# Forgetting attention's logits: two float32 heads side by side against stacked float32r halves

## The chip, the cores and the metric

The kernel runs on one core of one Trainium2 chip. The metric is the time of one execution on the device in microseconds (us), taken as the median of several runs. One execution was recorded by the hardware profiler; all rows shown come from that one.

## The reference

Four layers work on 256 tokens of width 1024, batch 1: two of a first block (gated linear attention, stick-breaking attention, each with an MLP) and two of a second block. The change lies in the second block, whose layers mix with eight heads of forgetting attention and eight heads of retention, each 64 wide. All data is float32.

```python
def forgetting_attention(q, k, v, f_logit):          # 8 heads of 64, 256 tokens
    log_f = jax.nn.log_sigmoid(f_logit)
    cum = jnp.cumsum(log_f, axis=1).transpose(0, 2, 1)
    ...
    logits = jnp.einsum('bhqd,bhkd->bhqk', qb, k) * HEAD_DIM ** -0.5
    logits = logits + cq[..., :, None] - cum[..., None, :]
    logits = jnp.where(kpos[None, :] <= qpos[:, None], logits, -jnp.inf)
    probs = jax.nn.softmax(logits, axis=-1)
    return jnp.einsum('bhqk,bhkd->bhqd', probs, v)
```

In each layer `u = rms_norm(h)`, `proj = u @ w_in` gives q, k, v, the forget logits and the retention's inputs, and `h + concat(fox, ret) @ w_out` follows.

## The kernel before

**Projections.** Activations lie feature by feature: a tile of 128 partitions holds 128 features of all 256 tokens. Every large product is made from float32r halves: a float32 operand x is split into `hi = float32r(x)` (a copy on ScalarE, ACT) and `lo = x - hi` (a subtraction on VectorE, DVE), and `mm3` (lines 402 to 404) issues three matmuls hi·hi, hi·lo, lo·hi. One call of `proj` walks eight steps k; a step is two output blocks of three matmuls, so six matmuls of 256 columns, and a call is 48. Weights come by DMA on SP's queue; `prep` splits each half of a weight (L330 on ACT, L333 on DVE, 128x1024 each) ahead of its use, in three buffered weights, with its priority pushed back by 150 (`LATER`).

**Hooks.** `proj(..., hooks=...)` calls functions between its steps, which puts small work of the attention between the matmuls of the next projection. `hooked("10 13 22 25", (f0, f1, f2, f3), 4)` says for each function two digits: how many projections after its own it runs, and behind which step. In forgetting attention one projection j (0 to 3) makes q and k of two heads (a pair).

**The order of the work.** The code's order is not the final one. Each instruction gets a priority in the order in which it is written, and when the program is built the framework's scheduler deals out each engine's instructions one after another: among those whose operands it estimates to be ready, the one with the best priority. The order of each engine, TensorE (PE) too, is then fixed, and the engine waits where an operand is later than estimated. `add_manual_dep` is used in places to hold an order against this.

**The pair, stage by stage.** `f0(j)` (L1117, L1118) reads q and k of the pair from PSUM, multiplies by the norm's reciprocal R (and q by -1/8) and writes them as float32 into `foxq`: head 0 in partitions 0 to 63, head 1 in 64 to 127. `f1(j)` (L1128) makes the logits: for each head, queries 0 to 127 against 128 keys and queries 128 to 255 against 256 keys, as float32 matmuls with 64 rows of contraction, the two heads in the two halves of the array's rows. Then come the row minimum of the negated logits with the decay added (L1136, DVE), exponentials with their sums (L396, ACT), the reciprocal and the scaling (L1139, L1141, DVE). `f2(j)` transposes the weights on PE (L1149) and copies them out (L1151, ACT); `f3` at every second pair multiplies by v and splits the result for `w_out`. While the first pair of a layer is worked on, the end of the retention part (`g2(1)`: L508 to L515, L1099, L1100, and the split L467, L468) is still on DVE and ACT.

**Buffers.** `SHARE` groups tile names into rings of buffers; `ga` has three of 640 float32 per partition and holds, among others, `foxl` (the logits); `gd` three of 512 with `foxq`; `gc` two of 512.

Of the kernel before, what the change touches and what calls it, by code (L numbers as in the profile page):

```python
# [11 lines left out]
F32R = mybir.dt.float32r  # L12
AF = mybir.ActivationFunctionType
ALU = mybir.AluOpType

P = 128
T = 256
# [202 lines left out]
class Net:  # L220
# [52 lines left out]

    SHARE = {}
    for _g, _n, _w, _names in (
        ("ga", 3, 640, "glaE sbe foxl relu pleg ffng retsq"),
        ("gb", 2, 640, "glaQ sbsp relu2 lnsq"),
        ("gc", 2, 512, "wa2 wa1 glaG sbh ph"),
        ("gd", 3, 512, "glasq qk foxq rot pl rgr"),
        ("ge", 1, 512, "retb ptin"),  # L280
        ("gf", 4, 384, "retw foxw sbw"),
        ("gg", 2, 512, "rety erz sbl w2 w2l"),
        ("gh", 2, 512, "lnq lnu ffny a1 glaK rgv rga"),
        ("gj", 2, 256, "sq rfv rfa"),
        ("gk", 2, 256, "diag lnvar"),
        ("gl", 2, 512, "lnsum retG"),
        ("gn", 1, 256, "lncm foxg idle"),
        ("go", 1, 256, "ssum foxf"),
        ("gr", 2, 256, "rfr"),
        ("gp", 2, 256, "spread"),  # L290
        ("gq", 1, 512, "retc glagrow"),
    ):
        for _x in _names.split():
            SHARE[_x] = (_g, _n, _w)
# [672 lines left out]
    def pv(self, v, c0, ws):  # L967
# [10 lines left out]
                    self.nc.tensor.matmul(pO[r, i // 2, P:T], v[:, 1, hc], ws[i][:, 256:384], start=False, stop=True, skip_group_check=True)  # L978
        return pO

    def diag0(self, a):

        d = a.rearrange("p (c n) -> p c n", n=P)
        for c in (0, 2):
            self.nc.gpsimd.affine_select(out=d[:, c, :], in_=d[:, c, :], pattern=[[1, P]], compare_op=ALU.is_gt, fill=0.0,
                                         base=0, channel_multiplier=-1)


    def mix2(self, l, x, acc):
        nc = self.nc  # L990
        mm = nc.tensor.matmul
# [14 lines left out]
        for c in range(2):  # L1006
            ps = rps[c]
# [4 lines left out]
        ps = self.proj(f"w_f{l}", 0, x)  # L1012
# [9 lines left out]
                                     op0=ALU.mult, op1=ALU.add)  # L1022

        gd = self.dram.tile([8, T], F32, name=f"cum{l}")
# [87 lines left out]
        fps, fqs, fls, fws = {}, {}, {}, {}  # L1112

        def f0(j):
            ps = fps[j]
            qk = self.t([P, 2, T], "foxq")
            nc.vector.scalar_tensor_tensor(out=qk[:, 0, :], in0=ps[:, 0, :], scalar=-0.125, in1=R, op0=ALU.mult, op1=ALU.mult)  # L1117
            nc.vector.tensor_tensor(out=qk[:, 1, :], in0=ps[:, 1, :], in1=R, op=ALU.mult)  # L1118
            fqs[j] = qk

        def f1(j):
            qk = fqs[j]

            pls = [self.pacc().rearrange("p a b -> p (a b)") for _ in range(2)]
            for a, b in ((0, 128), (128, 384)):
                for i in range(2):
                    r = slice(64 * i, 64 * i + 64)
                    mm(pls[i][:, a:b], qk[r, 0, a:a + P], qk[r, 1, 0:b - a], start=(a == 0), stop=True, skip_group_check=True)  # L1128
            fls[j] = []
            for i in range(2):  # L1130
                pl = pls[i]
                lg = self.t([P, 384], "foxl")
                mx = self.t([P, 2], "foxm")
                sm = self.t([P, 2], "foxs")
                for c, (a, b) in enumerate(((0, 128), (128, 384))):
                    nc.vector.tensor_tensor_reduce(out=lg[:, a:b], in0=pl[:, a:b], in1=fbs[j // 2][:, 2 * j % 4 + i, a:b], scale=1.0, scalar=3e38,  # L1136
                                                   op0=ALU.add, op1=ALU.min, accum_out=mx[:, c:c + 1])
                    self.act(lg[:, a:b], lg[:, a:b], "Exp", scale=-1.0, bias=mx[:, c:c + 1], accum_out=sm[:, c:c + 1])
                nc.vector.reciprocal(sm, sm)  # L1139
                for c, (a, b) in enumerate(((0, 128), (128, 384))):  # L1140
                    nc.vector.tensor_scalar(out=lg[:, a:b], in0=lg[:, a:b], scalar1=sm[:, c:c + 1], scalar2=None, op0=ALU.mult)  # L1141
                fls[j].append(lg)
# [16 lines left out]
        pv = self.proj_tok(f"w_fv{l}", 0, x, hooks=hk)  # L1159
        for c in range(2):  # L1160
            nc.scalar.mul(v[:, c, 0:512], pv[c].rearrange("p a b -> p (a b)"), rt[:, c:c + 1])
        fh = self.hooked("10 13 22 25", (f0, f1, f2, f3), 4)
        for j in range(4):
            fps[j] = self.proj(f"w_fqk{l}", j, x, hooks=([(3, lambda: g2(1))] if j == 0 else []) + fh(j))
        return o, (fh(4), fh(5), ())
# [272 lines left out]
```

## Time and profile before

| | before |
|---|---|
| median of 3 runs | 1303.39 us (1301.37 to 1304.65) |
| the profiled execution's own time | 1302.13 us |
| its span, first to last instruction | 1300.4 us |
| PE busy (matmuls) | 1282.7 us, 99% |
| PE weight loads busy | 1236.5 us, 95% |
| DVE busy | 946.8 us, 73% |
| ACT busy | 750.8 us, 58% |
| granted TensorE clock, mean | 0.998 |
| mean DMA rate | 179 GB/s |

The profiled execution's own time holds 1.7 us beside its span. A matmul's row gives its start and a duration that reaches past the start of the next one, since matmuls are pipelined: what a matmul costs is read from start to start, not from its duration. PEld are the weight loads of the same lines. A row of the timeline merges like instructions that follow each other (x8); in brackets stands how long the engine was idle before it, and what ended that.

### The profile page before, as it was taken

How to read it: one execution, taken by the hardware profiler on the slowest of the kernel's cores; microseconds unless marked ns; L12 is line 12 of the kernel's file. 1: busy time of each engine (PE TensorE's matmuls, PEld its weight loads, DVE VectorE, ACT ScalarE, POOL GpSimd, SP SyncE). 2: the span in 40 equal slices, each digit the busy share in tenths (PEclk: the TensorE clock that was granted, in tenths of full speed). 3: DMA queues.
4: the chain of work that ended last, by engine and by line, in shares of the span. 5: the costliest groups of instructions: out<-in, count | busy, mean ns of one | idle time of the engine just before them, and what ended most of it. 6: DMA issues, size and time to landing. Idle time of an engine off the chain costs nothing.

```text
span 1300.4 us, 25420 instructions
## 1 busy us (share of the span) xinstructions
PE 1282.7 (99%) x10314; PEld 1236.5 (95%) x10314; DVE 946.8 (73%) x1514; ACT 750.8 (58%) x1181; POOL 36.2 (3%) x89
## 2 busy tenths in 40 slices
PE   8999999999999999999999999999999999999997
PEld 6999999999899999999989999999989899999996
DVE  6979855559557955558887788766787869885755
ACT  6556744447776744446746665544674557554544
POOL 0000000000231000000010000000001000000000
PEclk9999999999999999999999999999999999999999
DMA  8654666654533575555654465565657446656561
GB/s 288 217 172 155 193 197 183 189 179 141 185 115 118 171 228 189 185 189 194 215 182 140 138 207 187 183 184 158 220 167 221 141 127 196 192 185 188 170 222 50
DMA packets 64694, 232.78 MB, mean 179 GB/s; under 512 B 7216, under 2 KB 7488, under 8 KB 63936
## 3 DMA queue, kind: packets, MB, share of 16 engines
q1 hardware_dynamic: 61920, 220.75, 54.1%
q10 hardware_dynamic: 2016, 8.28, 1.7%
q0 software_dynamic: 640, 2.11, 0.5%
q8 instruction: 81, 1.33, 0.4%
q14 instruction: 37, 0.30, 0.1%
HBM read 227.96 MB, written 3.16 MB: 178 GB/s over the span
## 4 chain that ended last, share of the span: by engine, by line
PE 90%; DVE 5%; DMA 3%; ACT 2%; issue 1%; POOL 0%; SPq 0%; POOLq 0%; ACTq 0%; DVEq 0%
PE up L402 20%; PE up L403 19%; PE up L404 19%; PE acc L403 9%; PE acc L404 8%; PE acc L402 8%; DVE wl L333 1%; DMA raw<-in_w_pg_dram 1%; PE aux L976 1%; ACT wh L330 1%; DMA wa<-in_w_a_dram 1%; PE aux L586 1%; PE acc L1128 1%; PE acc L1070 0%; DMA raw<-in_w_gv_dram 0%
## 5 line engine op out<-in xcount | busy, mean ns | idle before, releaser
L333 DVE TENSOR_TENSOR wl<-raw,wh 128x1024 fp32r<-128x1024 f32 (+2 forms) x420 | 506.3, 1210 | 257.1 <-ACT wh L330 255.4
L330 ACT CAST wh<-raw 128x1024 fp32r<-128x1024 f32 (+2 forms) x420 | 434.9, 1036 | 387.3 <-PE acc L403 139.2
L402 PE MATMUL up<-b,wh 128*128 128x256 f32 (+1 forms) x2032 | 576.2, 284 | 2.8 <-DVE pleg L1266 1.6
L403 PE MATMUL up<-b,wh 128*128 128x256 f32 (+1 forms) x2032 | 572.4, 282 | 0.2 <-DVE b L527 0.2
L404 PE MATMUL up<-b,wl 128*128 128x256 f32 (+1 forms) x2032 | 569.6, 280 | 0.0
L402 PEld LDWEIGHTS up<-b,wh 128*128 128x128 f32 x2032 | 381.5, 188 | 10.3 <-issue 5.2
L403 PEld LDWEIGHTS up<-b,wh 128*128 128x128 f32 x2032 | 382.8, 188 | 1.2 <-DVE b L527 0.4
L404 PEld LDWEIGHTS up<-b,wl 128*128 128x128 f32 x2032 | 382.9, 188 | 0.2 <-issue 0.2
L403 PE MATMUL acc<-b,wh 128*128 128x256 f32 (+1 forms) x960 | 270.6, 282 | 0.0
L404 PE MATMUL acc<-b,wl 128*128 128x256 f32 (+1 forms) x960 | 270.4, 282 | 0.0
L402 PE MATMUL acc<-b,wh 128*128 128x256 f32 (+1 forms) x960 | 270.2, 281 | 0.0
L402 PEld LDWEIGHTS acc<-b,wh 128*128 128x128 f32 x960 | 181.1, 189 | 0.1
L403 PEld LDWEIGHTS acc<-b,wh 128*128 128x128 f32 x960 | 181.0, 189 | 0.1
L404 PEld LDWEIGHTS acc<-b,wl 128*128 128x128 f32 x960 | 180.7, 188 | 0.1
L402 PE MATMUL up<-wh,b 128*128 128x512 f32 (+1 forms) x136 | 52.9, 393 | 1.6 <-ACT wh L361 1.6
L403 PE MATMUL up<-wl,b 128*128 128x512 f32 (+1 forms) x136 | 51.9, 381 | 0.0
L404 PE MATMUL up<-wh,b 128*128 128x512 f32 (+1 forms) x136 | 51.7, 381 | 0.0
L467 ACT CAST b<-ffny 128x256 fp32r<-128x256 f32 x44 | 17.9, 407 | 54.3 <-DVE ffny L1202 53.4
L402 PEld LDWEIGHTS up<-wh,b 128*128 128x128 f32 x136 | 25.5, 188 | 8.2 <-ACT wh L361 2.3
L404 PEld LDWEIGHTS up<-wh,b 128*128 128x128 f32 x136 | 25.5, 188 | 5.3
L403 PEld LDWEIGHTS up<-wl,b 128*128 128x128 f32 x136 | 25.6, 188 | 4.9 <-DVE wl L362 0.4
L1194 DVE TENSOR_TENSOR glaS<-up,rfr 128x256 f32<-128x256 f32 x44 | 18.7, 425 | 12.4 <-PE up L404 12.3
(257 smaller groups left out, 1151.3 us busy)
## 6 DMA issues: line engine op xcount, KB each, us to landing
raw<-in_w_fu_dram SPq DMA_DIRECT2D x88, 512.0 KB, 4.2
raw<-in_w_mu_dram SPq DMA_DIRECT2D x64, 512.0 KB, 4.1
raw<-in_w_md_dram SPq DMA_DIRECT2D x64, 512.0 KB, 4.2
raw<-in_w_fd_dram SPq DMA_DIRECT2D x32, 512.0 KB, 3.7
raw<-in_w_sqk_dram SPq DMA_DIRECT2D x16, 512.0 KB, 4.1
raw<-in_w_rqk_dram SPq DMA_DIRECT2D x16, 512.0 KB, 4.9
raw<-in_w_fqk_dram SPq DMA_DIRECT2D x16, 512.0 KB, 4.4
raw<-in_w_out_dram SPq DMA_DIRECT2D x16, 512.0 KB, 3.8
```

Of the source, the lines that this page charges most:

```text
L330: i = nc.scalar.copy(hi, r).ins
L333: i = nc.vector.tensor_tensor(out=lo, in0=r, in1=hi, op=ALU.subtract).ins
L402: mm(o, wh, xh, start=first, stop=False, skip_group_check=True)
L403: mm(o, wh, xl, start=False, stop=False, skip_group_check=True)
L404: self.last_mm = mm(o, wl, xh, start=False, stop=last, skip_group_check=True).ins
L467: nc.scalar.copy(out[0][:, i, :], src)
L586: nc.tensor.matmul(ps[:, k, :], ones, s[k][:, i, :], start=(k == 0 and i == 0), stop=(i == 1), skip_group_check=True)
L976: self.nc.tensor.matmul(pO[r, i // 2, :], v[:, 0, hc], ws[i][:, 0:256], start=(i < 2), stop=False, skip_group_check=True)
L1128: mm(pls[i][:, a:b], qk[r, 0, a:a + P], qk[r, 1, 0:b - a], start=(a == 0), stop=True, skip_group_check=True)
L1194: nc.vector.tensor_tensor(out=a[:, 2:], in0=ps[:, 0, :], in1=R, op=ALU.mult)
```

## The change

Each pair's q and k are written as before, in the order k, q, into a tile z. A new function `stack` makes for each of the two heads a tile X of 128 partitions and three slots in float32r: slot 0 has the high half of k in the head's own 64 partitions and the low half in the other 64; slot 1 has the high half of q in both; slot 2 the low half of q in both. A matmul of slot 1 against slot 0 contracts over 128 rows and gives q_hi·k_hi + q_hi·k_lo, one of slot 2 against slot 0 gives q_lo·k_hi + q_lo·k_lo. `f1` sums the two in PSUM, one head after the other. Hooks of f1 and f2 move by one step, and three names change rings.

```diff
-        ("ga", 3, 640, "glaE sbe foxl relu pleg ffng retsq"),
+        ("ga", 3, 768, "glaE sbe stack relu pleg ffng retsq"),
-        ("gc", 2, 512, "wa2 wa1 glaG sbh ph"),
-        ("gd", 3, 512, "glasq qk foxq rot pl rgr"),
+        ("gc", 2, 512, "wa2 wa1 glaG sbh foxq ph"),
+        ("gd", 3, 512, "glasq qk foxl rot pl rgr"),
...
+    def stack(self, z):
+        nc = self.nc
+        Xs = []
+        for i in range(2):
+            r, q = slice(64 * i, 64 * i + 64), slice(64 - 64 * i, 128 - 64 * i)
+            X = self.t([P, 3, T], "stack", F32R)
+            nc.scalar.copy(X[r, 0:2, :], z[r, :, :])
+            nc.vector.tensor_tensor(out=X[q, 0:3:2, :], in0=z[r, :, :], in1=X[r, 0:2, :], op=ALU.subtract)
+            nc.scalar.copy(X[q, 1, :], z[r, 1, :])
+            nc.vector.tensor_tensor(out=X[r, 2, :], in0=z[r, 1, :], in1=X[r, 1, :], op=ALU.subtract)
+            Xs.append(X)
+        return Xs
...
-            qk = self.t([P, 2, T], "foxq")
-            nc.vector.scalar_tensor_tensor(out=qk[:, 0, :], in0=ps[:, 0, :], scalar=-0.125, in1=R, op0=ALU.mult, op1=ALU.mult)
-            nc.vector.tensor_tensor(out=qk[:, 1, :], in0=ps[:, 1, :], in1=R, op=ALU.mult)
-            fqs[j] = qk
+            z = self.t([P, 2, T], "foxq")
+            nc.vector.tensor_tensor(out=z[:, 0, :], in0=ps[:, 1, :], in1=R, op=ALU.mult)
+            nc.vector.scalar_tensor_tensor(out=z[:, 1, :], in0=ps[:, 0, :], scalar=-0.125, in1=R, op0=ALU.mult, op1=ALU.mult)
+            fqs[j] = self.stack(z)
...
-            pls = [self.pacc().rearrange("p a b -> p (a b)") for _ in range(2)]
-            for a, b in ((0, 128), (128, 384)):
-                for i in range(2):
-                    r = slice(64 * i, 64 * i + 64)
-                    mm(pls[i][:, a:b], qk[r, 0, a:a + P], qk[r, 1, 0:b - a], start=(a == 0), stop=True, skip_group_check=True)
+            pls = []
+            for X in fqs[j]:
+                pl = self.pacc().rearrange("p a b -> p (a b)")
+                for a, b in ((0, 128), (128, 384)):
+                    for k in (1, 2):
+                        mm(pl[:, a:b], X[:, k, a:a + P], X[:, 0, 0:b - a], start=(a == 0 and k == 1), stop=(k == 2), skip_group_check=True)
+                pls.append(pl)
...
-        fh = self.hooked("10 13 22 25", (f0, f1, f2, f3), 4)
+        fh = self.hooked("10 14 23 25", (f0, f1, f2, f3), 4)
```

## Rows read from the trace of the kernel before

**Rows 1.** The page, the chain that ended last, by engine.

```profile
PE 90%; DVE 5%; DMA 3%; ACT 2%; issue 1%; POOL 0%; SPq 0%; POOLq 0%; ACTq 0%; DVEq 0%
```

**Rows 2.** One line's instructions: the logits' matmuls.

```profile
L1128 PE MATMUL acc<-foxq x64: 272/374/378, 691.8 to 1055.9; 64*128 64x128 f32 x32, 64*128 64x256 f32 x32
```

**Rows 3.** Timeline of PE around the logits of pairs 0 and 1, first layer.

```profile
691.55 0.28 PE L404 MATMUL up<-b,wl 128*128 128x256 f32 x1
691.76 0.93 PE L1128 MATMUL acc<-foxq 64*128 64x128 f32 x8
...
692.84 0.28 PE L403 MATMUL up<-b,wh 128*128 128x256 f32 x1
...
699.20 0.93 PE L1128 MATMUL acc<-foxq 64*128 64x128 f32 x8
```

**Rows 4.** Timeline of PE: 24 projection matmuls, then four float32 ones (L1096).

```profile
682.23 0.28 PE L402 MATMUL up<-b,wh 128*128 128x256 f32 x1
...
684.95 0.28 PE L404 MATMUL up<-b,wl 128*128 128x256 f32 x1
685.06 1.02 PE L1096 MATMUL aux<-retsq,tab 128*128 128x256 f32 x4
...
686.04 0.28 PE L403 MATMUL up<-b,wh 128*128 128x256 f32 x1
```

**Rows 5.** Timeline of PE around four matmuls of one column each (L486).

```profile
624.49 0.28 PE L404 MATMUL up<-b,wl 128*128 128x256 f32 x1
...
624.61 0.50 PE L486 MATMUL aux<-tab,ssum 128*128 128x1 f32 x4
...
625.17 0.28 PE L403 MATMUL up<-b,wh 128*128 128x256 f32 x1
```

**Rows 6.** Groups by line over the whole span: copies and subtractions.

```profile
L467 ACT CAST b<-relu 128x512 fp32r<-128x512 f32 x32 | 19.5, 617 | 0.5 <-DVE relu L712 0.5
L468 DVE TENSOR_TENSOR b<-relu,b 128x512 fp32r<-128x512 f32 x32 | 21.8, 686 | 0.6 <-ACT b L467 0.6
L467 ACT CAST b<-ffny 128x256 fp32r<-128x256 f32 x44 | 17.9, 407 | 54.3 <-DVE ffny L1202 53.4 <-issue 0.9
L1151 ACT COPY foxw<-acc 128x384 f32<-128x384 f32 x16 | 6.9, 484 | 12.8 <-PE acc L1149 12.8
```

**Rows 7.** Timeline of DVE, pair 0 of the first layer.

```profile
690.45 0.42 DVE L1118 TENSOR_TENSOR foxq<-up,spread 128x256 f32<-128x256 f32 x1
690.78 0.68 DVE L1099 TENSOR_TENSOR rety<-rgr,rety 128x512 f32<-128x512 f32 x1
691.38 1.22 DVE L333 TENSOR_TENSOR wl<-raw,wh 128x1024 fp32r<-128x1024 f32 x1
692.52 0.69 DVE L1100 TENSOR_TENSOR rety<-rety,retG 128x512 f32<-128x512 f32 x1
```

**Rows 8.** Timeline of DVE, pairs 1 and 2 of the first layer.

```profile
697.68 1.22 DVE L333 TENSOR_TENSOR wl<-raw,wh 128x1024 fp32r<-128x1024 f32 x1
700.15 0.29 DVE L1136 CUSTOM_DVE_ANT_0 foxl<-acc,b 128x128 f32<-128x128 f32 x1 [1.26 <-PE acc L1128]
...
704.19 1.22 DVE L333 TENSOR_TENSOR wl<-raw,wh 128x1024 fp32r<-128x1024 f32 x1
707.63 0.29 DVE L1136 CUSTOM_DVE_ANT_0 foxl<-acc,b 128x128 f32<-128x128 f32 x1 [2.22 <-PE acc L1128]
```

**Rows 9.** Timeline of DVE, pair 3 of the first layer, pair 0 of the second.

```profile
716.54 0.29 DVE L1136 CUSTOM_DVE_ANT_0 foxl<-acc,b 128x128 f32<-128x128 f32 x1 [2.14 <-PE acc L1128]
...
1031.27 1.22 DVE L333 TENSOR_TENSOR wl<-raw,wh 128x1024 fp32r<-128x1024 f32 x1
```

**Rows 10.** Timeline of PE in the second layer, around the spread of the norm.

```profile
964.18 0.28 PE L402 MATMUL up<-b,wh 128*128 128x256 f32 x1
965.62 0.68 PE L496 MATMUL aux<-diag,tab 128*128 128x128 f32 x4 [1.16 <-DVE diag L495]
966.05 0.36 PE L403 MATMUL up<-b,wh 128*128 128x256 f32 x1
```

More of the change, by code (lines that the diff above doesn't have):

```diff
@@ L1115, in f0 @@
             ps = fps[j]
-            qk = self.t([P, 2, T], "foxq")
-            nc.vector.scalar_tensor_tensor(out=qk[:, 0, :], in0=ps[:, 0, :], scalar=-0.125, in1=R, op0=ALU.mult, op1=ALU.mult)
-            nc.vector.tensor_tensor(out=qk[:, 1, :], in0=ps[:, 1, :], in1=R, op=ALU.mult)
-            fqs[j] = qk
+            z = self.t([P, 2, T], "foxq")
+            nc.vector.tensor_tensor(out=z[:, 0, :], in0=ps[:, 1, :], in1=R, op=ALU.mult)
+            nc.vector.scalar_tensor_tensor(out=z[:, 1, :], in0=ps[:, 0, :], scalar=-0.125, in1=R, op0=ALU.mult, op1=ALU.mult)
+            fqs[j] = self.stack(z)
         def f1(j):
-            qk = fqs[j]
-            pls = [self.pacc().rearrange("p a b -> p (a b)") for _ in range(2)]
-            for a, b in ((0, 128), (128, 384)):
-                for i in range(2):
-                    r = slice(64 * i, 64 * i + 64)
-                    mm(pls[i][:, a:b], qk[r, 0, a:a + P], qk[r, 1, 0:b - a], start=(a == 0), stop=True, skip_group_check=True)
+            pls = []
[5 more added lines that the diff above has]
+                pls.append(pl)
             fls[j] = []
```

## Prediction, made before the change was run

> **What bounds the kernel now.** I read the chain that ended last first: PE holds 90% of it, nothing else more than 5% [rows 1]. So what counts is time that PE spends or waits, and the change touches one line of it: the logits, 64 matmul records over both layers [rows 2]. The timeline of PE comes next, because a matmul's cost is the distance from start to start. Last come the timelines of DVE and ACT around the pairs, because the change gives these two more to do between the projection of a pair and its logits, and there it is open whether PE has to wait.
>
> **PE's own part.** Projection matmuls of 256 columns follow each other every (684.95 - 682.23) / 23 = 0.118 us [rows 4]. Around the logits of a pair the step from the last projection matmul to the second one after them is 692.84 - 691.55 = 1.29 us [rows 3]; without the logits it would be two paces, 0.24. So a pair costs PE 1.05 us before, eight records (two for each of four float32 products).
>
> What would these cost one after another? Four float32 records of 256 columns over the full array take 686.04 - 684.95 - 0.24 = 0.85 us, 0.21 each [rows 4]; by columns one of 128 takes 0.11. Four and four: 1.28 us, more than the 1.05 measured. So the two heads do run side by side now, some 0.64 us of streaming, and 0.41 goes to getting in and out (0.21 from the last projection matmul to the first record, where 0.118 is the pace [rows 3]). The stacked form gives the side by side away, and halves the passes: no gain from the streaming itself, only from the 0.41.
>
> After the change a pair is eight float32r matmuls over the full array: four of 256 columns at 0.118, and four of 128 columns, for which no row of before exists. Bounds: by columns half of 0.118, 0.059; at the price of a whole float32 product of 128 columns, two records of 0.11, 0.21. The nearest row is another: four matmuls of a single column, each with its own 128 columns of weights, take 625.17 - 624.49 - 0.24 = 0.44 us, 0.11 each [rows 5]. Whatever is streamed, a new set of weights costs 0.11. I take 0.11. A pair is then 4 x 0.118 + 4 x 0.11 = 0.91 us against 1.05: 0.14 less, **1.1 us less over eight pairs**. The bounds: 4 x 0.059 gives 0.71 and 2.7 us less in all; 4 x 0.21 gives 1.31 and 2.1 us more.
>
> The Trainium skill (TensorE: Matmul & The Clock Gate, Back-to-back issue gap) gives about 81 ns for a weight load and a matmul of 128 columns in a stream. By it a pair would be 4 x 0.081 + 0.47 = 0.80 us, an estimate, and the kernel 2.0 us faster; the one-column row above speaks for 0.11 in float32, and no run here has yet shown a float32r matmul of 128 columns.
>
> **What DVE and ACT get.** f0's two multiplications stay, in another order: nothing. `stack` adds, for each head, a copy of 64x512 and one of 64x256 on ACT (0.62 and 0.41 us, taken as 128 partitions [rows 6]) and two subtractions on DVE. A DVE operation of 512 columns occupies 691.38 - 690.78 = 0.60 us from start to start, one of 256 columns 690.78 - 690.45 = 0.33 [rows 7]. Per pair that is 1.86 us on DVE and at most 2.06 on ACT, some 15 and 16 us over eight pairs, on engines that are not the chain. DVE stood idle before the logits of pairs 1, 2 and 3 for 1.26, 2.22 and 2.14 us [rows 8, 9], and the hook of f1 comes one step (six matmuls, 0.71 us) later, so the 1.86 fits into 1.97, 2.93 and 2.85. The weight splits (L333) are three weights ahead and can slide. If that cover were gone, a pair would cost up to 1.86.
>
> f2 moves with f1, so the softmax keeps its seven steps. From f2 to f3 only two steps remain, 1.4 us, plus f1's 0.9 where it lies between; two copies of 0.48 [rows 6] lie there: nothing. The rings: X takes two of three buffers, free again as soon as its own logits are made, a whole projection before the next but one needs it; `foxl` leaves `ga` for a ring of three as before: nothing.
>
> **The wait that is new.** f1 needs X. From the start of the second multiplication the shortest chain is 0.42 + 0.62 + 0.60 + 0.42 = 2.06 us for head 0, 0.93 more for head 1, which is due half a pair (0.46) later. In pair 0 that start was at 690.45 and f1 at 691.76 [rows 3, 7]; with 0.71 more there are 2.02 us. And there DVE is full: L1099, then L333 for 1.14 us, then L1100 [rows 7]. That L333 sits between two dependent operations shows that the scheduler fills any gap with weight splits, and stack's first gap (the copy on ACT) is such a gap. With this order the subtractions begin at 692.52 + 0.60 = 693.12, those of head 1 end at 693.12 + 0.60 + 0.33 + 0.60 + 0.42 = 695.07, or 0.60 later with the split of `rety` (L468) among them. Head 1's passes were due at 691.76 + 0.71 + 0.46 = 692.93. X is 2.1 to 2.7 us late in pair 0, and the second layer has the same L333 at the same place [rows 9]. In pair 1 L333 goes first as well [rows 8]: 697.68 + 1.14 + 1.95 = 700.77 against 699.20 + 1.17 = 700.37, 0.4 late. Pair 2 has 704.19 + 1.14 + 1.95 = 707.28; its f1 was 0.95 before 707.63 (as 700.15 - 699.20 in pair 1), so head 1 is due at 707.85: in time, pair 3 likewise.
>
> Does PE stand still for these 2.1 to 2.7 us? In the second layer the spread's matmuls (L496) lie between the first and second matmul of one `mm3` [rows 10], where no hook stands. So PE's order too was dealt out by estimated readiness, and a late f1 will be set behind further projection matmuls. What is then late is the softmax of pair 0, which has seven steps (5 us) before its transposes, and these can be set back likewise. PE waits only where the estimate is too early. The same rows price that: 1.16 us, once. I take 0.3 for pair 0 of each layer, between nothing and 1.16.
>
> **Sum:** -1.1 + 0.6 = -0.5 us. On the profiled execution's own 1302.13 (its span of 1300.4 and 1.7 around it) that is 1301.6. The median of the runs lies 1.26 higher: **1302.9 us**.
>
> **The rivals.**
> - *As forecast, hidden* (0.74): from -2.7 to +1.2 us (1.16 in both first pairs), 1300.7 to 1304.6.
> - *PE stands and waits for X* (0.14): f1 stays at its hook, or the estimate is as early as that. Then 2 x (2.1 to 2.7 + 0.4) = 5.0 to 6.2 us of waits, less 1.1: +3.9 to +5.1, 1307.3 to 1308.5. For it: the wait at L496 [rows 10] and a full DVE in pair 0. Against: L496's own place. It is slower than before by over 0.3% once the waits pass 5.0 us in total.
> - *Short passes cost as float32* (0.08): +2.1 + 0.6, about 1306. Against it: the one-column row.
> - *The short passes cost by columns, and the new order saves other waits too* (0.04): -2.7 and one wait of 1.16 [rows 10]: 1299.5.
>
> The Trainium skill (VectorE: DVE Perf Modes, Two Vector instructions with no wait between them) says that an operation writing at another start partition than the one before it starts only when that one has finished. L1099 overlaps L333 by 0.08 us [rows 7]; without that overlap a pair's four subtractions would end 0.3 later, and the second case would be +4.5 to +5.7 us, an estimate.
>
> **From cases to chances.** 0.3% is 3.9 us, about what a measurement of this kernel can tell from no change. Faster: 0.02 of the first case, 0.03 of the last: 0.05. Slower: 0.02 of the first, 0.09 of the second, 0.01 of the third: 0.12. The rest, 0.83, within. The range takes in the first and third case with the runs' scatter (1301.37 to 1304.65) and ends where the second begins: 1299.8 to 1307.2.
>
> **What would show it right or wrong.** From the projection matmul before a head's four passes to the second one after them: 0.24 + 0.46 if the short pass is 0.11. The first f1 of each layer should lie some steps behind its hook with no PE idle before it; a PE wait on a subtraction of `stack` of 1 us or more in each layer is the second case. DVE should be fuller by 15 us. I am wrong if PE's order sticks to the hooks, or if weight splits pushed back by `stack` come late for `w_out`.

## The result, and the profile after

The changed kernel takes 1310.07 us (1308.73 to 1312.9, six runs) against 1303.23 us (1301.37 to 1304.65, six runs): ratio 1.0052, 95% interval 1.0041 to 1.0063. It is slower by 0.52%, 6.8 us; the prediction said 1302.9, a range of 1299.8 to 1307.2, and 0.12 for slower. The profiled execution's span is 1306.9 us for 1300.4, at a granted clock of 0.999 for 0.998, so the clock is not the difference.

The chain that ended last, by engine, in the profile after:

```profile
PE 85%; DVE 9%; DMA 3%; ACT 2%; issue 1%; POOL 0%; SPq 0%; POOLq 0%; DVEq 0%; ACTq 0%
```

In [rows 1] PE held 90% and DVE 5%: PE has lost five points of the chain and DVE has gained four. The new subtractions (L990) and the row minima behind them (L1152) are among its lines with 1% each, and the weight splits (L333) have gone from 1% to 2%.

**Where the time went.** The projection matmuls are the same in both kernels, in nearly the same order, so the k-th of one can be set against the k-th of the other. From the one before pair 0 to the one behind pair 3, the changed kernel falls back by 2.84 us in the first layer (0.92, 0.81, 0.76 and 0.35 by pair) and by 2.97 in the second. These 5.8 us are nearly all of the 6.5 between the spans; the rest is the net of +2.1 ahead of the first pair, -1.2 between the layers and -0.3 behind, where the code is the same. The six runs of the kernel before differ by 3.3 us among themselves. The count itself repeats well: a second trace of the kernel before without some weight splits (before_no_lo below) shows 0.00 in both layers.

**What PE does there.** PE's timeline after, pair 0 of the first layer; it answers to [rows 3]:

```profile
695.83 0.28 PE L404 MATMUL up<-b,wl 128*128 128x256 f32 x1
696.18 0.30 PE L1143 MATMUL acc<-stack 128*128 128x128 f32 x1
696.32 0.33 PE L402 MATMUL up<-b,wh 128*128 128x256 f32 x1
696.54 0.62 PE L1143 MATMUL acc<-stack 128*128 128x128 f32 x3
696.99 0.28 PE L403 MATMUL up<-b,wh 128*128 128x256 f32 x1
697.35 0.30 PE L1143 MATMUL acc<-stack 128*128 128x128 f32 x1
...
698.13 0.28 PE L403 MATMUL up<-b,wh 128*128 128x256 f32 x1
698.41 0.62 PE L1143 MATMUL acc<-stack 128*128 128x128 f32 x3
```

The eight matmuls have come apart into four pieces, dealt in among the projection's; in pair 1 it is the same. The steps ahead of the pieces are 0.35, 0.22, 0.36 and 0.28 us where the pace is 0.118 [rows 4]. In pairs 2 and 3 the eight stand together, but with steps of up to 0.37 us among them; this is the row of pair 2, which takes 1.08 us where nothing has to be waited for (x_const below):

```profile
711.33 1.68 PE L1143 MATMUL acc<-stack 128*128 128x128 f32 x8
```

Pair 0 on DVE answers to [rows 7]:

```profile
692.56 0.42 DVE L1133 SCALAR_TENSOR_TENSOR foxq<-up,spread 128x256 f32<-128x256 f32 x1
692.90 0.68 DVE L1114 TENSOR_TENSOR rety<-rgr,rety 128x512 f32<-128x512 f32 x1
693.50 1.22 DVE L333 TENSOR_TENSOR wl<-raw,wh 128x1024 fp32r<-128x1024 f32 x1
694.63 0.69 DVE L1115 TENSOR_TENSOR rety<-rety,retG 128x512 f32<-128x512 f32 x1
695.35 0.68 DVE L990 TENSOR_TENSOR stack<-foxq,stack 64x512 fp32r<-64x512 f32 x1
696.06 0.42 DVE L992 TENSOR_TENSOR stack<-foxq,stack 64x256 fp32r<-64x256 f32 x1
696.51 0.69 DVE L990 TENSOR_TENSOR stack<-foxq,stack 64x512 fp32r<-64x512 f32 x1
697.23 0.69 DVE L468 TENSOR_TENSOR b<-rety,b 128x512 fp32r<-128x512 f32 x1
697.93 0.42 DVE L992 TENSOR_TENSOR stack<-foxq,stack 64x256 fp32r<-64x256 f32 x1
698.39 0.29 DVE L1152 CUSTOM_DVE_ANT_0 foxl<-acc,b 128x128 f32<-128x128 f32 x1
```

Each piece starts just behind the subtraction that it needs: these end at 696.03, 696.48, 697.20 and 698.35, the pieces start at 696.18, 696.54, 697.35 and 698.41. So PE stands and waits for X, here four times in one pair. The list of PE's waits has one of them, 0.2 us. The view of the logits' line alone, which takes in PE's weight loads, shows more (both layers together; time in us, number of waits; "issue" is time in which the engine waited for nothing that the profile shows):

```profile
  issue: 1.7, 6
  DVE stack L992: 1.2, 6
...
  DVE stack L990: 0.2, 1
```

Even that is about half of what was lost: a matmul's row reaches to 0.28 behind its start, so a step of 0.35 leaves 0.07 that counts as idle. The whole of it is seen from start to start. Some of the loss stands at the transposes (L1165), with steps of up to 0.39 us ahead of them.

**How full DVE is.** Windows of the pairs, first before (pairs 0 to 3 of the first layer) and then after; columns are the window, its length, and the busy time of PE, PEld, DVE, ACT and POOL, each with its instructions, then clock, DMA share and GB/s:

```profile
688.70:696.00 7.30, 7.30 (x63) 6.83 (x62) 7.27 (x19) 4.82 (x12) 0.00 (x0) 1.00 0.45 152
696.00:703.50 7.50, 7.50 (x65) 7.04 (x65) 6.24 (x24) 4.93 (x13) 0.00 (x0) 1.00 0.49 141
703.50:711.00 7.50, 7.50 (x68) 6.44 (x67) 5.28 (x19) 4.80 (x13) 0.00 (x0) 1.00 0.47 143
711.00:718.50 7.50, 7.50 (x65) 7.04 (x65) 4.72 (x14) 4.71 (x12) 0.00 (x0) 1.00 0.42 137
```

```profile
690.80:698.90 8.10, 7.94 (x62) 7.29 (x61) 7.90 (x16) 5.49 (x8) 0.00 (x0) 1.00 0.44 133
698.90:707.00 8.10, 7.96 (x64) 7.35 (x63) 7.94 (x29) 6.82 (x21) 0.00 (x0) 1.00 0.24 67
707.00:714.80 7.80, 7.53 (x64) 6.63 (x65) 7.64 (x24) 6.49 (x17) 0.00 (x0) 1.00 0.45 139
714.80:722.40 7.60, 7.54 (x66) 7.11 (x63) 7.44 (x20) 6.53 (x15) 0.00 (x0) 1.00 0.66 199
```

Before, DVE was full beside pair 0 alone, with 1.3, 2.2 and 2.8 us free beside the others. After, it has 0.2 us free beside each. Over the whole span it is 74% busy, up from 73%.

### The profile page after: what moved, and what is told of

Same layout as the page of the kernel before. It is cut to its first block, busy times and chain, and to the rows that moved or that the text cites. A ratio compares the mean times of both kernels' runs of the same rounds, so it can differ in the third digit from the quotient of the medians.

```text
span 1306.9 us, 25480 instructions
## 1 busy us (share of the span) xinstructions
PE 1287.6 (99%) x10314; PEld 1241.7 (95%) x10314; DVE 963.9 (74%) x1546; ACT 765.5 (59%) x1213; POOL 35.9 (3%) x89
## 4 chain that ended last, share of the span: by engine, by line
PE 85%; DVE 9%; DMA 3%; ACT 2%; issue 1%; POOL 0%; SPq 0%; POOLq 0%; DVEq 0%; ACTq 0%
PE up L402 18%; PE up L403 18%; PE up L404 18%; PE acc L403 9%; PE acc L404 9%; PE acc L402 9%; DVE wl L333 2%; DVE stack L990 1%; PE aux L976 1%; ACT wh L330 1%; DMA wa<-in_w_a_dram 1%; PE aux L586 1%; DMA raw<-in_w_gg_dram 1%; DVE foxl L1152 1%; DMA raw<-in_w_gqk_dram 1%
## 5 line engine op out<-in xcount | busy, mean ns | idle before, releaser
L333 DVE TENSOR_TENSOR wl<-raw,wh 128x1024 fp32r<-128x1024 f32 (+2 forms) x420 | 506.0, 1208 | 252.9 <-ACT wh L330 251.1
```

The source lines that it names most:

```text
L333: i = nc.vector.tensor_tensor(out=lo, in0=r, in1=hi, op=ALU.subtract).ins
```

## The experiments

Letters in the expectations: theory **D**, DVE is full in this stretch, and what is put into it there is passed on to PE; **W**, PE waits for X because X is made too late behind its projection, whatever else DVE does; **P**, the new passes cost PE more than forecast; **A**, ACT's copies; **F**, the logits' falling apart into pieces; **L**, as D, seen from the softmax: scaled logits come late for the transposes. "Loss" below is the lag of the projection matmuls that a layer's four pairs add, against the kernel before, as above. Ratios go against runs of the kernel before on the same chip.

| kernel | median, us | ratio, 95% interval | loss, layers 1 and 2, us |
|---|---|---|---|
| changed | 1310.07 | 1.0052 [1.0041, 1.0063] | +2.84, +2.97 |
| x_const | 1303.23 | 0.9997 [0.9984, 1.0009] | -0.52, -0.51 |
| stack_unused | 1307.52 | 1.0029 [1.0017, 1.0041] | +1.93, +2.10 |
| late | 1313.44 | 1.0069 [1.0056, 1.0082] | +3.87, +4.02 |
| no_shift | 1308.48 | 1.0032 [1.0020, 1.0044] | +1.74, +1.85 |
| dve_only | 1310.14 | 1.0047 [1.0033, 1.0061] | +3.90, +2.59 |
| act_only | 1304.60 | 1.0000 [0.9987, 1.0012] | +0.34, +0.50 |
| pool_sub | 1337.64 | 1.0251 [1.0232, 1.0270] | +15.67, +16.84 |
| rows3 | 1304.46 | 1.0007 [0.9996, 1.0017] | +0.64, +0.77 |
| after_no_lo | 1306.14 | 1.0015 [1.0006, 1.0024] | +1.29, +1.48 |
| before_no_lo | 1303.21 | 0.9998 [0.9989, 1.0007] | 0.00, 0.00 |
| gather | 1308.73 | 1.0037 [1.0024, 1.0049] | +2.67, +2.82 |
| after_no_lo2 | 1303.94 | 1.0010 [0.9998, 1.0021] | +0.54, +0.69 |

**PE's passes alone (x_const).** The new matmuls on one constant tile, nothing made by `stack`, hooks and `foxl`'s ring as in the change (`ga` is as wide as before):

```diff
-            fqs[j] = self.stack(z)
+            fqs[j] = self.constX()   # one float32r tile, written once
```

> f1 multiplies a constant tile in float32r instead of the stacked halves, and stack is left out, so the logits don't come from q and k; number, form and place of PE's passes are those of the changed kernel. If PE's waits for the pieces of X are what costs (theory W), a pair takes 0.92 us of PE (4 x 0.118 and 4 x 0.11) against 1.05 before, and the kernel comes out 1 us below before, near 1302. If the float32r passes themselves are dear, fresh weights and 128 columns (rival P), a pair still takes 1.4 to 2.0 us and the time stays at 1306 to 1310.

PE's timeline of x_const, pair 0 of the first layer:

```profile
692.93 0.28 PE L404 MATMUL up<-b,wl 128*128 128x256 f32 x1
693.05 1.08 PE L1134 MATMUL acc<-cX 128*128 128x128 f32 x8
...
694.09 0.28 PE L403 MATMUL up<-b,wh 128*128 128x256 f32 x1
```

694.09 - 692.93 - 0.24 = 0.92 us for the pair, against 1.05 before. Both layers come out 0.5 us ahead. P falls: PE's own part of the change, with its hooks and rings, is a gain, though 1.0 us is too little for the medians to show (0.9997).

**The stack alone (stack_unused)**, X made and not used, the logits in float32 from z:

```diff
-            fqs[j] = self.stack(z)
+            self.stack(z)
+            fqs[j] = z          # f1 as before the change
```

> stack is made as in the change, but the logits are the float32 matmuls of before on z, at the change's hooks: the load on DVE and ACT without anybody on PE waiting for X. W: a pair takes 1.05 us of PE as before, transposes may come a little late: 1303 to 1305. If the load alone is the cause, because softmax and transposes come late (rival L), most of the loss stays: 1307 to 1310.

No matmul needs X here, and yet each layer loses 2 us, as L forecast: W cannot be the whole. PE now waits visibly, 2.7 us in four waits, for the scaled logits (L1157) ahead of f2's transposes.

**Later hooks (late).**

```diff
-        fh = self.hooked("10 14 23 25", (f0, f1, f2, f3), 4)
+        fh = self.hooked("10 20 30 32", (f0, f1, f2, f3), 4)
```

> The change with f1 four steps later (20), f2 and f3 behind it (30, 32): X is complete before PE comes to it. W: the waits at the pieces of X go, a pair falls to about 0.92 us, 1302 to 1304. P: nothing moves, 1309 to 1311. L: the softmax is as late against its transposes as before, 1307 to 1310.

More time between the projection and its logits makes it worse, by 1 us a layer, and worse than any of the three forecasts. Waits for X are left (0.9 us in two), and others come up at the transposes (2.0 us) and at the products with v (1.5 us).

**ACT's and DVE's share, each by itself (act_only, dve_only)**, from stack_unused: the two subtractions of a head left out, or the two copies.

```diff
             nc.scalar.copy(X[r, 0:2, :], z[r, :, :])                                              # act_only
-            nc.vector.tensor_tensor(out=X[q, 0:3:2, :], in0=z[r, :, :], in1=X[r, 0:2, :], op=ALU.subtract)
...
-            nc.scalar.copy(X[r, 0:2, :], z[r, :, :])                                              # dve_only
+            nc.vector.tensor_tensor(out=X[q, 0:3:2, :], in0=z[r, :, :], in1=z[r, :, :], op=ALU.subtract)
```

> stack's four copies on ACT alone, result unused, logits in float32 as before at the change's hooks. D: ACT has room (6.8 of 8.1 us with the stack), 1303 to 1304.5. A: 1306 to 1307.5.

> stack's four subtractions on DVE alone (of z from itself, result unused; no copies on ACT), logits in float32 as before at the change's hooks. If a full DVE in this stretch is what costs (theory D: DVE was busy 7.9 of 8.1 us per pair in the changed kernel), this keeps nearly all that the whole unused stack cost, +2.5 to +4 us over before: 1306 to 1307.5. If it is the hand-over between ACT and DVE or ACT's own load (rival A), it is near before: 1303 to 1304.5.

The copies cost nothing that the ratio can show, 0.3 to 0.5 us a layer at most: A falls. The subtractions by themselves, whose results nobody reads and which wait for no copy, carry the loss. (The median, 1310.14, is above D's forecast; about 1.7 us of the first layer's 3.90 come from a lower granted clock, shown in the last section.) Where it arises is seen in PE's timeline of dve_only at the transposes of the first layer's last pair (in brackets PE's idle time):

```profile
723.05 0.61 PE L1163 MATMUL acc<-tab,foxl 128*128 128x128 f32 x3 [1.45 <-DVE foxl L1155]
...
723.92 0.86 PE L1163 MATMUL acc<-tab,foxl 128*128 128x128 f32 x3 [0.27 <-DVE foxl L1155]
```

In this layer the first three pairs lost only 0.16 us together; the debt fell due at the end of the last.

**Without changing start partitions (no_shift)**, all of `stack` on 128 partitions from partition 0, as many DVE and ACT operations of the same widths (one of the two subtractions shown; the copy of q goes to a tile of its own):

```diff
-            nc.vector.tensor_tensor(out=X[q, 0:3:2, :], in0=z[r, :, :], in1=X[r, 0:2, :], op=ALU.subtract)
+            nc.vector.tensor_tensor(out=X[:, 0:3:2, :], in0=z, in1=X[:, 0:2, :], op=ALU.subtract)
```

> stack with the same number and width of operations, but every one on 128 partitions from partition 0, so none writes at another start partition than the one before; both heads' halves then hold mixed rows and the logits are not those of the reference. If an operation that changes start partitions can't overlap the one before (part of W), the subtractions follow each other at 0.60 and 0.33 us instead of 0.72 and 0.45, X is complete 0.48 us earlier per pair, and 2 to 4 us of the loss go: 1306 to 1308. If that overlap doesn't matter, 1309 to 1311. P: 1309 to 1311.

DVE's timeline after the change, pair 3, has the four subtractions in a row:

```profile
719.38 0.69 DVE L990 TENSOR_TENSOR stack<-foxq,stack 64x512 fp32r<-64x512 f32 x1
720.10 0.42 DVE L992 TENSOR_TENSOR stack<-foxq,stack 64x256 fp32r<-64x256 f32 x1
720.55 0.69 DVE L990 TENSOR_TENSOR stack<-foxq,stack 64x512 fp32r<-64x512 f32 x1
721.27 0.42 DVE L992 TENSOR_TENSOR stack<-foxq,stack 64x256 fp32r<-64x256 f32 x1
721.72 0.29 DVE L1152 CUSTOM_DVE_ANT_0 foxl<-acc,b 128x128 f32<-128x128 f32 x1
```

and no_shift the same work as two runs of two:

```profile
716.29 1.29 DVE L989 TENSOR_TENSOR stack<-foxq,stack 128x512 fp32r<-128x512 f32 x2
717.50 0.76 DVE L991 TENSOR_TENSOR stack<-foxq,stack 128x256 fp32r<-128x256 f32 x2
```

In the changed kernel they start 0.72 and 0.45 us apart, in no_shift and before [rows 7] 0.60 and 0.33: 2.34 us a pair in place of 1.86. The third of the four writes from partition 0 like the second and only reads from another start, 64, and it too comes 0.45 behind. Without that 0.48 the layers lose 1.74 and 1.85, 1.1 less each; the median, 1308.48, lies between the two forecasts.

**On GpSimd (pool_sub)**, `nc.vector` to `nc.gpsimd` in the two subtractions:

> The change with stack's four subtractions on GpSimd instead of DVE; all else and the result as in the change. D: DVE carries what it carried before; f1 still waits for X, on an engine that is 3% busy, whose pace for 64x512 no row shows yet; at some 1 us each PE sets f1 later and the time is 1303 to 1306. If the waits at X's pieces cost by themselves (W), it stays at 1308 to 1312.

The groups of pool_sub by line:

```profile
L990 POOL TENSOR_TENSOR stack<-foxq,stack 64x512 fp32r<-64x512 f32 x16 | 25.0, 1560 | 109.3 <-ACT stack L989 108.7
L992 POOL TENSOR_TENSOR stack<-foxq,stack 64x256 fp32r<-64x256 f32 x16 | 15.3, 958 | 1.2
```

GpSimd needs 1.56 and 0.96 us in the mean where DVE needs 0.69 and 0.42; PE waits 16.8 us for it in 20 waits, and the two layers lose 32.5 us, far more than either forecast. A part of that is the granted clock, 0.68 to 1.00 over ten-microsecond stretches of these layers. DVE is freed, but X comes later still: here W is the bound.

**Less splitting (rows3)**, the two heads side by side as before the change, one high and one low tile for both, three passes (the product of the two low halves left out; `ga` has four buffers of 640):

```diff
+            nc.scalar.copy(hi, z)
+            nc.vector.tensor_tensor(out=lo, in0=z, in1=hi, op=ALU.subtract)
...
+                for k, (q, kk) in enumerate(((hi, hi), (hi, lo), (lo, hi))):
```

> Another form of the logits: z of both heads is split once over 128 partitions (one copy and one subtraction of 512 columns per pair), and the heads stay side by side in the array's halves with three passes hi.hi, hi.lo, lo.hi; the term lo.lo is left out. DVE gets 0.60 us per pair instead of 2.3, ACT 0.5. By rows of before PE streams 3 x 384 columns side by side, 0.48 us, plus 0.41 to get in and out: 0.89 against 1.05. D: 1302 to 1304, the same as before or a little better. W: X is still one subtraction away, a wait in the first pair of each layer: 1304 to 1306.

One subtraction of 512 columns a pair is left on DVE, 0.60 us in place of 2.34, and most of the loss is gone with it. What is left stands in pairs 0 and 1 (0.57 of 0.64 and 0.68 of 0.77), and the median lies in W's forecast, 0.5 above D's. Pairs 2 and 3 together add 0.07 and 0.09, so the twelve matmuls take PE no less than the eight before, and not the 0.89 us expected. It does not beat the kernel before, and no version run here that computes the logits does.

**Less of DVE's other work (after_no_lo, before_no_lo).** The weight subtractions (L333) of the output weights, eight a layer, which stand among the stack's:

```diff
-            i = nc.vector.tensor_tensor(out=lo, in0=r, in1=hi, op=ALU.subtract).ins
+            if not name.startswith("w_out"):      # else lo is hi
+                i = nc.vector.tensor_tensor(out=lo, in0=r, in1=hi, op=ALU.subtract).ins
```

> The changed kernel with the subtraction that makes the low half of an output weight left out (the low half is the high half again, so the output projection is wrong); these are the 1.2 us weight subtractions of VectorE that stand among the stack's in the forgetting-attention stretch. Theory D (VectorE is full there, so every 1.2 us in front of a stack or a scaled logit is passed on to TensorE): up to 2.4 us of 7.9 a pair fall away, VectorE is at some 6 of 8, and most of the 5.8 us of the two stretches comes back: 1302 to 1305, ratio 0.999 to 1.002. Rival W (the matmuls wait because X is a chain of copy and subtraction behind the projection, whatever else VectorE does): 1307 to 1311, ratio 1.003 to 1.006, with the gaps of up to 0.36 us before the logits still there.

> The kernel before with the same weight subtractions left out (the same output projection is wrong). Theory D: VectorE had room there, so nothing comes back: 1302 to 1304, ratio 0.999 to 1.001. Rival (VectorE's weight splits delayed TensorE before the change as well, and leaving them out helps any kernel): 1297 to 1300, ratio 0.995 to 0.998; then a gain of the changed kernel would say nothing of the stack.

The same edit gives the kernel before nothing and the changed one more than half of its loss, all of it in pairs 1 to 3: after pair 0 the lag is 0.91 as it was, after pair 1 1.55 for 1.73, and pairs 2 and 3 give 0.26 back where they lost 1.1. Work on DVE that cost nothing before the change costs PE time after it. That is D: the ratio 1.0015 is in its range, with W's at 1.003 to 1.006, though the median, 1306.14, lies between the two ranges in us. What comes back is 3.0 of the 5.8 us, where D expected most of them.

**Pieces held together (gather)**, with an order for PE and no other change:

```diff
+                        self.tc.add_manual_dep(i, lsub[j].name, order, reason="order")   # i: each matmul of f1
```

> The changed kernel with all eight short matmuls of a pair ordered behind the last of its four subtractions, so that no piece of the logits is dealt in among the projection's matmuls while X is half made. Rival F (the loss is in the pieces: each waits a little and shows its weight load, 0.163 for 0.112): the pieces run back to back at 0.92 a pair, and 2 to 3 us come back: 1306 to 1308, ratio 1.002 to 1.004. Theory D: VectorE is as full as before, the logits only come later and the transposes wait for the scaled logits instead: 1309 to 1313, ratio 1.004 to 1.008.

The ratio, 1.0037, is in F's range, the median lies between the two theories' ranges, and the interval overlaps both ratio ranges and the changed kernel's: the time does not decide. The losses do: 2.67 and 2.82, some 0.15 less each. The eight matmuls now stand together, but PE still waits among them for the last subtraction (0.9 us listed in two waits on L992) and 1.3 us at the transposes. So F is worth 0.3 us at most where it acts; the rest of the difference in the medians is not accounted for.

**Still less of DVE's work (after_no_lo2)**, `startswith(("w_out", "w_fqk"))` in the same edit:

> As after_no_lo, with the low halves of the forgetting-attention projection's own weights left out as well (high halves twice, so that projection and the output projection are wrong): the last 1.2 us subtractions beside the first two pairs. After after_no_lo, pairs 2 and 3 of a layer cost nothing any more and 1.3 to 1.5 us a layer were left, all in pairs 0 and 1, where VectorE was still at 7.9 of 8.1. Theory D (the rest too is VectorE's load): the rest falls to between the -0.5 of x_const and +0.8 a layer, 1301.5 to 1304.5, ratio 0.998 to 1.0008. Rival W (the rest is the chain of copy and subtraction itself, which pair 0 has to wait for because nothing was made ahead): 1.2 to 1.5 a layer stay, 1305 to 1307, ratio 1.001 to 1.003.

Windows of after_no_lo2, the same stretches as before:

```profile
688.70:696.00 7.30, 7.09 (x55) 6.55 (x54) 7.09 (x15) 4.99 (x8) 0.00 (x0) 1.00 0.35 124
696.00:703.50 7.50, 7.50 (x65) 7.50 (x65) 6.19 (x27) 7.40 (x21) 0.00 (x0) 1.00 0.51 166
703.50:711.00 7.50, 7.50 (x67) 7.08 (x67) 5.79 (x23) 6.98 (x19) 0.00 (x0) 1.00 0.47 150
711.00:718.50 7.50, 7.50 (x70) 7.33 (x67) 5.37 (x17) 6.08 (x12) 0.00 (x0) 1.00 0.32 109
```

PE has no gap left in pairs 1 to 3, where DVE has 1.3 to 2.1 us free, and each of them now gains 0.06 to 0.15 us, about what PE's own part says. The loss is all in pair 0, 0.86 us in this layer and 0.97 in the other, where DVE is full (7.09 of 7.30) with the end of the retention part. The losses of 0.54 and 0.69 a layer and the median, 1303.94, are within D's forecast. The ratio, 1.0010, is just above D's 1.0008 and at the lower end of W's range, so the time alone would not decide between them.

The trace shows what stands in front of X in pair 0. DVE in after_no_lo2:

```profile
691.80 0.69 DVE L1116 TENSOR_TENSOR rety<-rety,retG 128x512 f32<-128x512 f32 x1
692.52 0.69 DVE L991 TENSOR_TENSOR stack<-foxq,stack 64x512 fp32r<-64x512 f32 x1
693.24 0.42 DVE L993 TENSOR_TENSOR stack<-foxq,stack 64x256 fp32r<-64x256 f32 x1
693.58 0.68 DVE L469 TENSOR_TENSOR b<-rety,b 128x512 fp32r<-128x512 f32 x1
694.28 0.69 DVE L991 TENSOR_TENSOR stack<-foxq,stack 64x512 fp32r<-64x512 f32 x1
```

ACT had the copies for the two L991 ready at 691.82 and 692.90, so they started 0.70 and 1.38 us behind their operands, each just behind an operation of the retention part (L1116, L469). The second layer shows the same order.

## Why the prediction was wrong

**PE's own part was right in its sum.** 0.91 us a pair was forecast, 0.92 measured; -1.1 us over the eight pairs against -1.03 in x_const's two layers. Taken off the sum, a float32r matmul of 128 columns costs (0.92 - 4 x 0.118) / 4 = 0.112 us, the one-column row's 0.11 [rows 5]. The single steps are not so even: in x_const they are 0.06 and 0.11 us behind the two matmuls of 128 columns of a head, 0.17 and 0.12 behind its two of 256. The sum, 0.115 for each of the eight, bears the prediction out; the split by width, 0.11 and 0.118, is not what the trace shows. By the Trainium skill's figure (TensorE: Matmul & The Clock Gate, Back-to-back issue gap), 81 ns for a matmul of 128 columns in a stream, the prediction's estimate for the pair was 0.80 us, which these matmuls don't reach.

**The step that failed is the one that cost DVE's new work at nothing**: "the 1.86 fits into 1.97, 2.93 and 2.85. The weight splits (L333) are three weights ahead and can slide." Three things in it were wrong.
- *Its size.* The subtractions take 2.34 us a pair. In the changed kernel and in no_shift the difference, 0.12 for each, follows the changing start partition. The Trainium skill (VectorE: DVE Perf Modes, Two Vector instructions with no wait between them) says that an instruction which reads or writes from another quadrant (32 partitions) than the last one did starts only when the earlier ones have finished. The traces agree: these start 0.03 us behind the end of the one before, where those of [rows 7] overlap by 0.08. The prediction had only the write, as 0.3 us a pair in a rival, and not in DVE's load; it is 0.48 a pair, and worth 1.1 us a layer.
- *What fills the idle time.* The idle time of [rows 8, 9] stood behind the weight splits, and the splits did not slide. In pair 0 L333 goes in front of X as it went in front of L1100 [rows 7]; with DVE full the stack, the softmax and the splits of every pair stand in one line. after_no_lo and its counterpart before_no_lo show that PE pays for splits in that line: without eight of them a layer gets 1.5 us back, where the kernel before gets nothing.
- *That room in a pair is room in time.* X and the scaled logits have their places in PE's fixed order, and in the changed kernel each small lateness is paid on the spot. The prediction checked X against its hook in pairs 2 and 3 and found it in time; these lost 0.76 and 0.35.

**The term for waits was mis-sized**: +0.6 us in all where it is 5.8 + 1.0 = 6.8, some 0.85 a pair. 0.3 a layer came from the belief that PE's order would be dealt around a late X. It was dealt around it, the four pieces among projection matmuls in pairs 0 and 1 show that, but by an estimate that is too early at each piece.

**The second case** ("PE stands and waits for X") was the nearest, +3.9 to +5.1. Its chain of DVE in pair 0 came true instruction by instruction, L333 and L468 included, only with each operation from the first subtraction on 0.10 to 0.12 later than the one before it allowed for. But it priced pairs 0 and 1 alone, X alone, and had 0.14. Its sign of recognition, a listed wait of 1 us or more on a subtraction of `stack`, would have missed it: the listed wait is 0.2 us.

**DVE fuller by 15 us** was forecast as what would show the step right. It is 17.1 us fuller (963.9 against 946.8). The forecast of the load was nearly right, the conclusion that it lies beside PE was wrong.

**What stays open.** after_no_lo2 still lies 1.1 to 1.2 us a layer above x_const. It arises in pair 0. Its trace puts the retention's operations on DVE, and not ACT's copies, in front of X there; no run leaves them out, so what they are worth is not shown. The effects of the changing start partitions and of the weight splits were each measured alone and do not add up.

## What to carry to other kernels

Before work on an idle engine is costed at nothing, take its busy time in the very stretch, add the new work at its real pace, and ask what stands in front of it in that engine's order: here 73% over the span stood beside 98% in the pairs once the work was in. Idle time behind deferrable work is not free for work that someone waits for, as long as the deferrable work goes first. Where a matmul stream is fed in small pieces, look for lost time in the steps from start to start, and in the weight loads' waits: of waits of 0.1 to 0.25 us the list for PE had a single one.

## What the runs showed of the hardware

A wait can be followed by a loss as large as itself. Windows of dve_only around its two waits of 1.45 and 0.27 us:

```profile
723.00:724.00 1.00, 0.69 (x4) 0.45 (x4) 0.84 (x4) 1.00 (x3) 0.00 (x0) 1.00 0.83 311
724.00:725.00 1.00, 1.00 (x5) 0.94 (x6) 0.81 (x2) 0.74 (x3) 0.00 (x0) 0.52 0.09 37
725.00:726.00 1.00, 1.00 (x6) 1.00 (x6) 0.45 (x1) 0.30 (x1) 0.00 (x0) 0.50 0.00 0
726.00:727.00 1.00, 1.00 (x7) 1.00 (x5) 0.00 (x0) 0.00 (x0) 0.00 (x0) 0.50 0.42 98
727.00:728.00 1.00, 1.00 (x8) 0.60 (x9) 0.00 (x0) 0.00 (x0) 0.00 (x0) 0.77 0.82 287
```

Behind them the granted clock is 0.50 for some three microseconds, the lower of the two levels (1.2 in place of 2.4 GHz), and PE, busy throughout, does half its work: about 0.48 + 0.50 + 0.50 + 0.23 = 1.7 us lost, as much again as the waits. Without them this layer would be at 2.2, where the other shows 2.59 at a clock of 1.00, with waits that add up to as much (1.7 us in two) at the same place. So this was seen once in two, and what decides it is not shown. In the changed kernel the clock stayed at 1.00 in the four windows of its pairs.
